# Small matrix products ahead of a recurrence, spread over parts of the TensorE array

## The chip, the cores and the metric

One core of a Trainium2 chip runs the whole program in one launch. The metric is the device time of an execution in microseconds (us). The engines are TensorE (PE; its weight loads are shown as PEld), VectorE (DVE), ScalarE (ACT), GpSimd (POOL) and SyncE (SP, which issues most of the transfers).

## What is computed

Two layers of an encoder on 768 tokens of width 1024 (a prompt of 512 and a sample of 256). Layer 0 runs differential attention and a bidirectional RWKV-7 time mixing side by side; layer 1 is a dilated sliding-window attention; each layer ends in a feed-forward part. The change lies in the time mixing. Its core in the reference, for 8 heads of width 64, once forwards and once backwards:

```python
def icl_rate(a0, a1, a2):
    return jax.nn.sigmoid((a0 + (xa @ a1) @ a2).astype(f32))

def step(st, inp):
    r_t, w_t, k_t, v_t, kk_t, a_t = inp
    sa = jnp.einsum('bhvk,bhk->bhv', st, -kk_t)
    st = (st * w_t[:, :, None, :] + sa[..., None] * (kk_t * a_t)[:, :, None, :]
          + v_t[..., None] * k_t[:, :, None, :])
    y = jnp.einsum('bhvk,bhk->bhv', st, r_t)
    return st, y
```

The decay `w_t` and the rate `a_t` come from two-stage ("low-rank") gates of the tokens.

## The kernel before

**The recurrence in chunks.** The kernel cuts the 768 tokens into 12 chunks of 64. Within a chunk the steps of the scan become matrix products, if the inverse of a unit triangular 64x64 matrix is at hand for every chunk, head and direction. `rkv` prepares all that for four pairs of heads (pair j, heads at partitions 0 to 63 and 64 to 127), and `rwkv` runs the recurrence later from what was stored to DRAM.

**For each pair and direction** (`operand_set`, j = 0 to 3, "f" then "b"): `stage` makes the second stage of the decay's and the rate's gate, two products each (512 and 256 tokens), in the PSUM bank `st`, each with a sigmoid on ACT (L671). `operands` makes the chunk operands on DVE and POOL, among them KB (L606) and AL (L608, L609). `store` sends them to DRAM. `products` makes A = KB^T AL per chunk and head, a 64x64 product (L632), six of one head in the one bank `pr`; ACT copies the 32x32 diagonal blocks into G (L645) and the other block into AO (L648). One more product in `pr`, `bonus`, ends a pair.

**The inverses** (`invert`) are made in three groups of 16 (pair, chunk) for both heads and directions: group 0 holds pair 0 and chunks 0 to 3 of pair 1, group 1 reaches to chunk 7 of pair 2, group 2 to the end of pair 3. DVE turns G into M (L729 forwards, L730 backwards), and then inverts 128 blocks of 32x32 at once, row after row: a multiplication (L737) and a sum (L739) for each, 48 of each in a group, a strict chain. Four transposes (L750, L751) end a group; L751 writes into M's memory. ACT and POOL copy them into TS, Tif and Tib (L769). Then PE makes the block off the diagonal: for each direction and head 16 products of 32x32 of AO with TS in the one bank `iv`, a copy to Hs (L774), 16 more of Hs with Ti, and a copy into Ti (L779), eight batches with a copy behind each. The result goes to DRAM.

**What sets the order.** PE has much else to do meanwhile: the projections of r, k, v, of the attention's values and of its q and k, in bank `gm` (line L83, three products in float32r for one exact product). The program is written in plain order; the scheduler of the Tile framework puts each engine's instructions into one fixed order by its own reckoning at build time, so an engine waits at the next instruction of its list even if a later one could run. The eight PSUM banks are given out by use: `iv` 1, `gm` 4, `uv` 1, `st` 1, `pr` 1.

In the code below, `self.mm` is a matrix product (L83 or, for plain float32, L84), `self.bank(tag)` takes the next PSUM bank of a use, `P` is 128.

## Time and profile before

| | us |
|---|---|
| three runs | 2135.32, 2132.63, 2128.2 |
| median | 2132.63 |
| span of the profiled execution | 2132.5 |
| PE busy | 2047.4 |
| DVE busy | 1392.7 |
| ACT busy | 906.3 |
| POOL busy | 882.1 |

In the span, the products of `pr` lie between 103 and 337 us, those of `iv` between 271 and 475, and the recurrence begins at 502. "Busy" sums up the instructions of an engine; a stretch of the span has to be looked at by itself, since the engines' loads differ from stage to stage. In a row of a timeline the bracket at the end tells how long the engine stood idle before it and what it was then released by. PE's rows are its matrix products; `x12` means twelve records one after another, and a float32 product has two records, a float32r one has one.

### The profile page before, as it was taken

The numbers are of one execution on the slowest core, as the hardware profiler recorded it, in microseconds if no ns is written. First come the engines' busy times: TensorE is split into PE (matmuls) and PEld (weight loads), VectorE is DVE, ScalarE is ACT, GpSimd is POOL, SyncE is SP. The second block draws the span as 40 slices with busy tenths as digits, with TensorE's granted clock in tenths as the row PEclk, the third lists the DMA queues.
The fourth block names the chain that finished last, engine by engine and source line by source line (L and its number), as shares of the span: only waits on it lengthen the run. The fifth ranks groups of instructions, "written<-read, shape, count | busy, mean of one in ns | idle before, by whom it ended". The sixth has DMA issues, their size and how long they took to land. (4 is left out here: it accounts for less than half of the span.)

```text
span 2132.5 us, 33757 instructions
## 1 busy us (share of the span) xinstructions
PE 2047.4 (96%) x13270; PEld 1775.0 (83%) x13270; DVE 1392.7 (65%) x2147; ACT 906.3 (43%) x1703; POOL 882.1 (41%) x833
## 2 busy tenths in 40 slices
PE   7999999999998989999999999999998999999998
PEld 7767666777887779999999998888677999999997
DVE  5456987956679567566666667643567666666665
ACT  5467555356655254433333334222454433333332
POOL 3345331552113157543434535443137544543442
PEclk9999989998999999999999999999998999999999
DMA  4334325114356312211221235221121121111124
GB/s 155 84 78 92 90 65 162 43 26 132 95 165 179 124 51 79 79 60 60 77 72 70 76 132 195 71 70 39 50 109 60 62 87 70 69 70 60 60 80 148
DMA packets 150228, 189.01 MB, mean 89 GB/s; under 512 B 95927, under 2 KB 107785, under 8 KB 150069
## 3 DMA queue, kind: packets, MB, share of 16 engines
q1 hardware_dynamic: 126880, 168.00, 24.6%
q10 hardware_dynamic: 20372, 12.03, 2.0%
q0 software_dynamic: 2816, 6.83, 1.0%
q8 instruction: 104, 1.70, 0.3%
q14 instruction: 56, 0.45, 0.1%
HBM read 150.20 MB, written 36.23 MB: 87 GB/s over the span
## 5 line engine op out<-in xcount | busy, mean ns | idle before, releaser
L83 PE MATMUL gm<-xh,w 128*128 128x384 f32 x896 | 249.6, 343 | 2.9 <-ACT xh L139 2.9
L140 DVE TENSOR_TENSOR wl<-wraw,wh 128x1024 fp32r<-128x1024 f32 (+1 forms) x96 | 128.0, 1334 | 153.0 <-ACT wh L139 150.7
L83 PE MATMUL gm<-T,w 128*128 128x384 f32 x1032 | 203.8, 340 | 6.6 <-ACT w L139 6.0
L83 PE MATMUL gm<-xh,wh 128*128 128x256 f32 (+3 forms) x640 | 206.1, 346 | 1.2 <-ACT pad L489 0.8
L83 PE MATMUL gm<-xl,wh 128*128 128x256 f32 (+3 forms) x640 | 204.5, 345 | 0.0
L83 PE MATMUL gm<-xh,wl 128*128 128x256 f32 (+3 forms) x640 | 203.0, 344 | 0.0
L140 DVE TENSOR_TENSOR w<-S,w 128x512 fp32r<-128x512 f32 x176 | 168.5, 959 | 43.8 <-ACT w L139 36.3
L83 PEld LDWEIGHTS gm<-T,w 128*128 128x128 f32 x1032 | 184.3, 188 | 11.4 <-ACT w L139 7.2
L139 ACT CAST wh<-wraw 128x1024 fp32r<-128x1024 f32 (+1 forms) x103 | 107.5, 1045 | 163.0 <-PE gm L83 88.3
L139 ACT CAST w<-S 128x512 fp32r<-128x512 f32 x176 | 108.8, 621 | 155.0 <-POOL S L291 54.6
L83 PEld LDWEIGHTS gm<-xh,w 128*128 128x128 f32 x896 | 167.9, 192 | 7.8 <-ACT xh L139 3.5
L139 ACT CAST w<-wraw 128x512 fp32r<-128x512 f32 x126 | 76.5, 620 | 207.9 <-PE gm L83 138.3
L83 PE MATMUL gm<-xl,w 128*128 128x384 f32 x448 | 153.6, 343 | 4.0 <-DVE xl L140 4.0
L293 POOL TENSOR_TENSOR S<-wraw,S 128x512 f32<-128x512 f32 x42 | 62.8, 1496 | 204.5 <-DVE w L140 204.5
L140 DVE TENSOR_TENSOR w<-wraw,w 128x512 fp32r<-128x512 f32 x126 | 116.8, 944 | 39.6 <-ACT w L139 39.6
L83 PE MATMUL sc<-xh,w 128*128 128x384 f32 x512 | 140.8, 336 | 1.1 <-DVE u L330 1.1
L83 PEld LDWEIGHTS gm<-xh,wh 128*128 128x128 f32 (+1 forms) x640 | 119.0, 193 | 21.0 <-issue 4.9
L83 PEld LDWEIGHTS gm<-xl,wh 128*128 128x128 f32 (+1 forms) x640 | 118.3, 193 | 21.3 <-issue 9.1
L83 PEld LDWEIGHTS gm<-xh,wl 128*128 128x128 f32 (+1 forms) x640 | 118.5, 193 | 20.8 <-issue 7.9
L392 DVE TENSOR_TENSOR acc<-acc,ob 128x512 f32<-128x512 f32 x128 | 87.4, 683 | 67.0 <-PE ob L83 65.8
L83 PE MATMUL sc<-T,w 128*128 128x384 f32 x552 | 112.6, 343 | 6.0 <-DVE sil L330 2.6
L348 POOL TENSOR_TENSOR sil<-sil,v 128x384 f32<-128x384 f32 x44 | 46.9, 1065 | 163.3 <-DVE v L330 163.1
(502 smaller groups left out, 5312.1 us busy)
## 6 DMA issues: line engine op xcount, KB each, us to landing
wraw<-in_gate SPq DMA_DIRECT2D x44, 512.0 KB, 3.4
wraw<-in_down SPq DMA_DIRECT2D x44, 512.0 KB, 3.5
wraw<-in_up SPq DMA_DIRECT2D x40, 512.0 KB, 3.4
wraw<-in_wqk SPq DMA_DIRECT2D x20, 512.0 KB, 3.5
wraw<-in_wo SPq DMA_DIRECT2D x14, 512.0 KB, 4.1
wraw<-in_wrkv SPq DMA_DIRECT2D x12, 512.0 KB, 3.5
KB<-pkKB SPq DMA_DIRECT2D x24, 256.0 KB, 3.5
pkx<-x SPq DMA_DIRECT2D x12, 512.0 KB, 3.4
```

The costliest lines, as they stand in the source:

```text
L83: return self.nc.tensor.matmul(o, a, b, start=start, stop=stop)
L139: self.nc.scalar.copy(out=hi, in_=x)
L140: (eng or self.nc.vector).tensor_tensor(out=lo, in0=x, in1=hi.bitcast(F32), op=ALU.subtract)
L293: eng.tensor_tensor(out=s2, in0=a12, in1=s2, op=ALU.subtract)
L348: nc.gpsimd.tensor_tensor(out=o, in0=o, in1=a[0], op=ALU.mult)
L392: nc.vector.tensor_tensor(out=accs[t][:, fs], in0=accs[t][:, fs], in1=os[t, f], op=ALU.add)
```

## The change

It does three things in layer 0, none elsewhere.

1. `products`: six chunks of both heads fill one `pr` bank, head 0 and head 1 in turn, so that neighbouring products use different halves of the array's rows and columns. Two steps of 12 products replace four of 6. The copies are the same in number and size and follow behind both heads.
2. `invert`: the 64 products of a kind (16 for each direction and head) fill one `iv` bank in turn over the four, and Hs is copied once, from 128 partitions. The copies into Ti stay four.
3. `stage`: the decay's product for a split of the tokens is followed by the rate's for the same split, the first in bank `st`, the second in bank `pr`; the rate's weights and hidden rows are packed with the directions swapped, so that the two use different halves of the array's rows.

```diff
         def products(j, d, AL, RH, KB, KK):
             ba = 0 if d == "f" else 1
-            def step(par, c0, n):
-                rr = slice(64 * par, 64 * par + 64)
+            def step(c0, n):
                 b = self.bank("pr")
                 for c in range(n):
-                    self.mm(b[rr, c * 64:c * 64 + 64], KB[rr, c0 + c], AL[rr, c0 + c])
-                bv = b[:, 0:n * 64].rearrange("p (c t) -> p c t", t=64)
+                    for rr in (slice(0, 64), slice(64, P)):
+                        self.mm(b[rr, c * 64:c * 64 + 64], KB[rr, c0 + c], AL[rr, c0 + c])
+                for par in range(2):
+                    copies(b[:, 0:n * 64].rearrange("p (c t) -> p c t", t=64), par, c0, n)
+
+            def copies(bv, par, c0, n):
                 i = 12 * j + c0
...
-            for a in ((0, 0, 6), (1, 0, 6), (0, 6, 6), (1, 6, 6)):
-                step(*a)
+            for c0 in (0, 6):
+                step(c0, 6)
...
         def stage(j, d):
             di = "fb".index(d)
-            rr = slice(64 * di, 64 * di + 64)
-            out = []
-            for n, w, b0 in (("w", self.w2, "w0_"), ("a", self.a2, "a0_")):
-                x = tile("s" + n)
-                for s0, S in SPLIT:
-                    o = self.bank("st")
+            out = [tile("sw"), tile("sa")]
+            of = (("w", self.w2, "w0_", di, "st"), ("a", self.a2, "a0_", 1 - di, "pr"))
+            for s0, S in SPLIT:
+                os = [self.bank(tag) for *_, tag in of]
+                for o, (n, w, b0, half, _) in zip(os, of):
+                    rr = slice(64 * half, 64 * half + 64)
                     self.mm(o[:, :S], w[rr, j * P:(j + 1) * P], self.hid[n][rr, s0:s0 + S])
+                for x, o, (n, w, b0, *_) in zip(out, os, of):
                     nc.scalar.activation(out=x[:, s0:s0 + S], in_=o[:, :S], func=AF.Sigmoid, bias=col(b0 + d, j))
-                out.append(x)
             return out
...
+        hb = self.bank("iv")
+        for c in range(16):
+            for di, ba, bb, ra, rb in parts:
+                self.mm(hb[rb, c * 32:c * 32 + 32], AO[ra, c], TS[ra, c])
+        nc.scalar.copy(out=Hs.rearrange("p c t -> p (c t)"), in_=hb)
+        hb = self.bank("iv")
+        for c in range(16):
+            for di, ba, bb, ra, rb in parts:
+                self.mm(hb[ra, c * 32:c * 32 + 32], Hs[rb, c], Ti[di][rb, c, 32 * bb:32 * bb + 32])
         for di, ba, bb, ra, rb in parts:
-            hb = self.bank("iv")
-            for c in range(16):
-                self.mm(hb[rb, c * 32:c * 32 + 32], AO[ra, c], TS[ra, c])
-            nc.scalar.copy(out=Hs[rb].rearrange("p c t -> p (c t)"), in_=hb[rb])
-        for di, ba, bb, ra, rb in parts:
-            hb = self.bank("iv")
-            for c in range(16):
-                self.mm(hb[ra, c * 32:c * 32 + 32], Hs[rb, c], Ti[di][rb, c, 32 * bb:32 * bb + 32])
             nc.scalar.copy(out=Ti[di][ra, :, 32 * bb:32 * bb + 32], in_=hb[ra].rearrange("p (c t) -> p c t", c=16))
...
-    a["wla"] = cols_tile(np.concatenate([i["a1_f"], i["a1_b"]], 1))[0]
+    a["wla"] = cols_tile(np.concatenate([i["a1_b"], i["a1_f"]], 1))[0]
...
-    a["a2"] = np.concatenate([i["a2_f"], i["a2_b"]])
+    a["a2"] = np.concatenate([i["a2_b"], i["a2_f"]])
```

The remaining lines of the diff take comments away; line numbers move by three from `stage` on and by four behind `invert`. The scheduler's order of the whole of layer 0 moves with the change; in layer 1, from its feed-forward part on, it is the same. Numbers in the names below only tell tiles apart; line numbers are those of the kernel each piece comes from.

PE, before, the last products of pair 3 (`pr` from AL and KB, backwards) among the products of the third gate (`st`):

```order
L84 MATMUL pr_354_2737<-AL_348_2705,KB_350_2707 64x64 x6
L84 MATMUL st_395_3251<-g2a_494,hg_3167 128x512
L84 MATMUL st_395_3251<-pad0_280,hh_3234 128x512
L84 MATMUL pr_355_2747<-AL_348_2705,KB_350_2707 64x64 x6
L84 MATMUL st_397_3257<-g2a_494,hg_3167 128x512
L84 MATMUL st_397_3257<-pad0_280,hh_3234 128x512
L84 MATMUL pr_356_2757<-AL_348_2705,KB_350_2707 64x64 x6
L84 MATMUL st_399_3263<-g2a_494,hg_3167 128x512
L84 MATMUL st_399_3263<-pad0_280,hh_3234 128x512
L84 MATMUL pr_372_3042<-rk_277,kfb_352_2709 128x2 x6
```

PE, before, a little later, the first off-diagonal products of group 1 (`iv` from TS and AO) among projections (`gm`):

```order
L83 MATMUL gm_423_3411<-wh_410_3289,xh_2_89 128x512
L83 MATMUL gm_423_3411<-wl_411_3290,xh_2_89 128x512
L83 MATMUL gm_423_3411<-wh_410_3289,xl_3_90 128x512
L83 MATMUL gm_423_3411<-wh_410_3289,xh_2_89 128x512
L84 MATMUL iv_284_2212<-TS_280_2192,AO_175_1264 32x32 x16
L83 MATMUL gm_423_3411<-wl_411_3290,xh_2_89 128x512
L83 MATMUL gm_423_3411<-wh_410_3289,xl_3_90 128x512
```

So all of pair 3 stands ahead of group 1's off-diagonal products. PE after, at the same place:

```order
L84 MATMUL st_363_3214<-pad0_280,hh_3191 128x512
L84 MATMUL iv_266_2191<-TS_262_2171,AO_171_1266 32x32 x64
L84 MATMUL pr_327_2695<-AL_322_2673,KB_324_2675 64x64 x12
L84 MATMUL st_365_3220<-g2a_494,hg_3124 128x512
L84 MATMUL st_365_3220<-pad0_280,hh_3191 128x512
L83 MATMUL gm_389_3368<-wh_370_3234,xh_2_89 128x512
L83 MATMUL gm_389_3368<-wl_371_3235,xh_2_89 128x512
```

The first block of pair 3 backwards (`pr_327`) stands right behind the 64 products of group 1. PE after, the second block (`pr_328`) and what is ahead of it:

```order
L84 MATMUL iv_267_2257<-Tif_264_2173,Hs_263_2172 32x32 x2
L84 MATMUL iv_267_2257<-Tib_265_2174,Hs_263_2172 32x32 x2
L84 MATMUL pr_328_2714<-AL_322_2673,KB_324_2675 64x64 x12
L84 MATMUL st_367_3226<-g2a_494,hg_3124 128x512
L84 MATMUL st_367_3226<-pad0_280,hh_3191 128x512
```

It stands behind the second batch of group 1's off-diagonal products, the one that reads Hs.

DVE, before, from the last transposes of group 1 to the first rows of group 2:

```order
L750 STREAM_TRANSPOSE tm_279_2087<-X_278_2086 64x1024
L751 STREAM_TRANSPOSE M_277_2085<-X_278_2086 64x1024
L750 STREAM_TRANSPOSE tm_279_2087<-X_278_2086 64x1024
L751 STREAM_TRANSPOSE M_277_2085<-X_278_2086 64x1024
L679 COPY bon_79<-pr_372_3042 128x6x2
L729 STREAM_TRANSPOSE M_357_2767<-G_258_1979 64x1024
L730 STREAM_TRANSPOSE M_357_2767<-G_258_1979 64x1024
L737 TENSOR_TENSOR tm_359_2769<-X_358_2768,M_357_2767 128x1 x2
L739 TENSOR_REDUCE X_358_2768<-tm_359_2769 128x1 x2
```

DVE, after, at the same place:

```order
L753 STREAM_TRANSPOSE tm_261_2066<-X_260_2065 64x1024
L754 STREAM_TRANSPOSE M_259_2064<-X_260_2065 64x1024
L603 TENSOR_SCALAR kfb_326_2677<-sa_316_2654,cols_115,omka_272 128x768
L605 SCALAR_TENSOR_TENSOR sa_316_2654<-kk_276_2403,sa_316_2654 128x768
L732 STREAM_TRANSPOSE M_329_2733<-G_243_1967 64x1024
L606 TENSOR_TENSOR KB_324_2675<-sa_316_2654,sw_315_2653 128x768
L733 STREAM_TRANSPOSE M_329_2733<-G_243_1967 64x1024
L740 TENSOR_TENSOR tm_331_2735<-X_330_2734,M_329_2733 128x1 x2
L742 TENSOR_REDUCE X_330_2734<-tm_331_2735 128x1 x2
```

Between the transposes and M there now stand two instructions that lead to KB of pair 3 backwards (L603, L605), and KB itself (L606) between M's two halves.

PE, before, the last of the projections (`gm`) ahead of the recurrence, with the attention's transposes (`tr`) and scores (`sc`) behind:

```order
L83 MATMUL gm_683_4673<-xh_2_89,wh_685_4676 128x256
L83 MATMUL gm_683_4673<-xl_3_90,wh_685_4676 128x256
L83 MATMUL gm_683_4673<-xh_2_89,wl_686_4677 128x256
L87 MATMUL tr_487_3782<-ident_113,o2_483_3770 128x128 x3
L84 MATMUL iv_371_3020<-Tib_363_2877,Hs_361_2875 32x32 x16
L87 MATMUL tr_487_3782<-ident_113,o2_483_3770 128x128
L84 MATMUL sc_544_4052<-k_514_3865,q_512_3863 128x512
L84 MATMUL sc_544_4052<-l_515_3866,q_512_3863 128x512
```

PE, after, at the same place:

```order
L83 MATMUL gm_649_4630<-xl_3_90,wh_651_4633 128x256
L83 MATMUL gm_649_4630<-xh_2_89,wl_652_4634 128x256
L87 MATMUL tr_453_3739<-ident_113,o2_449_3727 128x128 x4
L84 MATMUL sc_515_4033<-k_479_3821,q_477_3819 128x512
L84 MATMUL sc_515_4033<-l_481_3823,q_477_3819 128x512
L84 MATMUL sc_517_4040<-k_480_3822,q_478_3820 128x512
L84 MATMUL sc_517_4040<-l_481_3823,q_478_3820 128x512
```

The last off-diagonal batch stood behind the last projection before and now stands far ahead of it. From the last projection to the recurrence's first product there are 43 rows between them before and 32 now.

## Rows read from the trace of the kernel before

**Rows 1.** the page, busy us with the share of the span, and instructions
```profile
PE 2047.4 (96%) x13270; PEld 1775.0 (83%) x13270; DVE 1392.7 (65%) x2147; ACT 906.3 (43%) x1703; POOL 882.1 (41%) x833
```

**Rows 2.** windows: stretch, us, busy PE, PEld, DVE, ACT, POOL, clock, DMA share, GB/s
```profile
0.00:204.00 204.00, 187.83 (x1100) 148.81 (x1101) 109.56 (x129) 115.28 (x201) 84.25 (x60) 0.97 0.39 104
204.00:262.00 58.00, 52.99 (x313) 40.06 (x313) 57.41 (x123) 30.68 (x60) 20.73 (x11) 0.91 0.33 73
262.00:290.00 28.00, 24.25 (x168) 17.55 (x169) 22.32 (x24) 21.16 (x36) 14.05 (x11) 0.79 0.46 117
290.00:338.00 48.00, 47.40 (x397) 32.16 (x397) 43.56 (x106) 22.93 (x43) 12.39 (x9) 0.98 0.39 84
338.00:352.00 14.00, 11.79 (x34) 6.76 (x32) 9.18 (x8) 11.21 (x13) 5.89 (x7) 0.63 0.37 117
352.00:428.00 76.00, 73.17 (x599) 59.29 (x599) 70.17 (x151) 30.03 (x42) 32.26 (x33) 1.00 0.27 86
470.00:502.00 32.00, 28.94 (x142) 20.68 (x141) 15.94 (x45) 14.34 (x41) 10.37 (x31) 0.68 0.27 75
```

**Rows 3.** groups of DVE, 204 to 428 us: names, shapes, count, busy us, mean ns
```profile
L737 DVE TENSOR_TENSOR tm<-X,M 128x1 f32<-128x1 f32 (+15 forms) x144 | 81.5, 593 | 1.0
L739 DVE TENSOR_REDUCE X<-tm 128x1 f32<-128x1 f32 (+15 forms) x144 | 43.4, 326 | 1.1
```

**Rows 4.** timeline of DVE at both hand-overs: start us, us, engine, line, operation
```profile
270.62 1.90 DVE L751 STREAM_TRANSPOSE M<-X 64x1024 f32<-64x1024 f32 x1
...
289.98 0.21 DVE L737 TENSOR_TENSOR tm<-X,M 128x1 f32<-128x1 f32 x2
...
342.69 1.91 DVE L751 STREAM_TRANSPOSE M<-X 64x1024 f32<-64x1024 f32 x1
...
349.52 1.24 DVE L729 STREAM_TRANSPOSE M<-G 64x1024 f32<-64x1024 f32 x1 [4.71 <-ACT TS L769]
...
352.12 0.23 DVE L737 TENSOR_TENSOR tm<-X,M 128x1 f32<-128x1 f32 x2
```

**Rows 5.** timeline of PE: small products, each with the next instruction
```profile
103.38 0.91 PE L84 MATMUL pr<-AL,KB 64*64 64x64 f32 x12
104.21 0.39 PE L83 MATMUL gm<-xh,wh 128*128 128x256 f32 x1
...
503.87 0.68 PE L84 MATMUL pp<-AL,KB 64*64 64x64 f32 x16 [0.78 <-DVE LR L968]
504.48 0.51 PE L84 MATMUL sc<-k,q 128*128 128x512 f32 x1
...
427.06 1.19 PE L84 MATMUL iv<-TS,AO 32*32 32x32 f32 x32
428.19 0.71 PE L84 MATMUL ob<-va,pT 128*128 128x128 f32 x4
```

**Rows 6.** timeline of PE: the first product of the recurrence
```profile
502.02 1.06 PE L84 MATMUL pp<-RH,KB 128*128 128x128 f32 x8
```

**Rows 7.** line 774, the Hs copies: min/median/max ns, first and last start
```profile
L774 ACT COPY Hs<-iv x12: 571/577/581, 279.2 to 450.2; 32x512 f32<-32x512 f32 x12
```

**Rows 8.** timeline of PE, behind the wait for AL of pair 0
```profile
132.39 1.54 PE L84 MATMUL pr<-AL,KB 64*64 64x64 f32 x12 [3.47 <-DVE AL L609]
133.86 1.22 PE L84 MATMUL st<-hw,w 64*128 64x256 f32 x2
...
142.10 0.28 PE L83 MATMUL gm<-xh,wh 128*128 128x256 f32 x1
142.22 0.39 PE L83 MATMUL gm<-xh,wl 128*128 128x512 f32 x1
142.46 0.28 PE L83 MATMUL gm<-xl,wh 128*128 128x256 f32 x1
```

**Rows 9.** timeline of ACT ahead of group 0
```profile
200.07 1.28 ACT L671 ACT_TABLE_LOAD   x1
...
202.08 0.79 ACT L645 COPY G<-pr 32x128 f32<-32x128 f32 x2
```

## The prediction

> **What bounds the kernel now.** I read the page's busy times first. TensorE (PE) is busy in 96% of the span [rows 1], so at first sight every microsecond taken from it comes back. That share is an average, and the change touches only the first 475 us, so I cut that part into stages with the windows view [rows 2]. Up to 204 us PE is the fullest engine, 187.8 of 204. From 204 to 428 us the 32-row inversions run on VectorE (DVE), three groups one after another: 57.4 of 58 us busy in the rows of group 0, 43.6 of 48 in group 1's, 70.2 of 76 in group 2's. PE is 84 to 99% busy there too, but with projections that no one awaits at once, and at 0.63 and 0.79 of its clock in the two stretches between the groups. The view of DVE's groups of instructions says what fills it: 144 multiplications and 144 reductions of the substitution, 124.9 us in one chain [rows 3]. So two things run side by side, a PE queue and a DVE chain, and what decides is which of them arrives last where they meet: at the products that feed a group (bank pr), and at the off-diagonal products behind it (bank iv).
>
> The DVE timeline shows the two hand-overs [rows 4]. Group 0's last transpose ends at 272.5 and the next group's rows start at 290.0: 17.5 us. Group 1's ends at 344.6 and the rows of group 2 start at 352.1: 7.5 us, 4.7 of it a wait for ScalarE's (ACT's) TS copies. This hand-over is short because the last products of pair 3 had long been made. Behind group 2 the iv products start at 427.06 [rows 5], the recurrence's first product at 502.02 [rows 6]. Of the 1630 us behind it the change alters nothing, and PE bounds them [rows 1], so the recurrence's start carries the end: a shift there is a shift of the time. The profiled span, 2132.5, and the median of the runs, 2132.63, agree, so the sum is made on 2132.5 and nothing is added around it.
>
> **What the change saves on PE.** *Products:* a block of 6 products (12 records) runs from 103.38 to the next instruction at 104.21, 0.83 us, 69 ns for a record with its share of the entry [rows 5]. There are 32 blocks: 26.6 us. The recurrence's own 64x64 products already alternate between heads: 16 records from 503.87 to 504.48, 0.61 us, 38 ns for a record [rows 5]. By that price 16 blocks of 24 records are 16 x 0.91 = 14.6 us, a gain of 12 (0, if they take turns, to 13, if the price is just half). *Off-diagonal products:* 32 records from 427.06 to 428.19, 1.13 us, 35 ns each; 24 blocks are 27.1 us. Four tiles now alternate. Nothing in [rows 5] shows four, so I bound it: no gain (27), halved once as with the two heads (about 13), or twice (7). I take 13, a gain of 14 (0 to 20). *ACT* saves 9 of 12 Hs copies, 9 x 0.577 = 5.2 us [rows 7]; ACT is half idle there [rows 2], so this counts as nothing by itself. *Stage:* the order on PE does not bring the two gates' products together: other products stand between w's (bank st) and a's (bank pr). Products that are not neighbours share nothing, so I give this 0. Its cost is that the one pr bank now serves 16 products of a more; that price lies in the first term below. In all 26 us (0 to 33) of PE's time, were it all on the path.
>
> The Trainium skill ("TensorEngine Tiling (Array Packing)", Gotcha 1: PSUM Pressure) says that different row tiles cannot access one PSUM bank at the same time, which would take the gain of the products away, since both heads still fill one bank. By that rule the 12 us would be 0. The recurrence's products of two heads at 38 ns [rows 5], made in one bank too, speak against it; it comes back as a rival.
>
> **Why I don't count that gain.** The whole order moves, so I follow the chain from station to station.
>
> 1. *Group 0's start (its first rows, at 204 us).* On PE the products ahead of it are 7 blocks of 24 records in place of 14 of 12: 14 x 0.83 less 7 x 0.91, 5.2 us saved. But the order puts 22 projections of 512 and 21 of 256 columns more ahead of it; by the 0.24 and 0.12 us from start to start in [rows 8] that is 5.3 + 2.5 = 7.8 us. Two products of the gates' second stage fewer stand ahead of it, one of 512 and one of 256 columns, some 2 us by the 1.22 of one of 256 at half clock [rows 8], so no net work is left on either side. What may be won: PE stood 3.47 us for AL of pair 0's backward direction, and at 132.39 the block took 1.54 in place of 0.91 us, half clock [rows 8]; this AL now comes earlier on DVE. What may be lost: the pr bank is waited for by a's sigmoids. I take -4 (between -9, the wait and the slow stretch behind it both gone, and +3, one ACT copy queue behind a sigmoid and its table load, 200.07 to 202.08, [rows 9]).
>
> 2. *Hand-over of group 0 to 1.* Before: 17.5 us. Now KB of pair 2's backward direction stands on DVE behind the group's last transposes, and both its product blocks stand on PE behind iv of group 0; G's copies follow, then M. The chain counted as in the next item is 20 to 22 us; I take +4 (0 to +6).
>
> 3. *Hand-over of group 1 to 2.* This is the largest term. Before: all of pair 3's products stand on PE ahead of group 1's iv, M could start as soon as the TS copies let go of it. Now, from the order: DVE makes KB of (pair 3, backward) behind the transposes; PE has 64 iv products, then the first block of (pair 3, backward), then the projections and 64 more iv products that wait for Hs, and only then the second block; ACT has Hs, six copies, three bank copies of other work, the Ti copies and then the six copies of that second block, for which M waits. Counted from the end of the last transpose: TS copies 4.9 us (344.6 to 349.52, [rows 4]); the first iv batch 2 to 4; Hs 0.6 [rows 7]; six copies at about 0.4 (0.39 for the two of [rows 9]) 2.4; three copies as wide as Hs 1.7, while PE does the products up to the second batch; four Ti copies as long as Hs's 2.3, later by up to 2 if the second batch is; six copies 2.4; a transpose of M 1.24 [rows 4]. That is 17.5 to 21.5 us in place of 7.5. I take 18.5, +11 (+6, if ACT's copies of other work hide in PE's time, to +14). DVE has KB's chain of about 4 us to do in it that before lay among the rows, and this comes off the rows: it is in the lower end.
>
> 4. *Group 2's end to the recurrence.* Before: 75 us, of which 470 to 502 is the tail of the attention, 32 us with PE at 0.68 of its clock and 3 us of gaps [rows 2]. iv's eight batches with a copy behind each are now two, and more projections are left for this stretch: the last of them stands 33 rows ahead of the recurrence's first product, 44 before. Behind it there are 12 scores of 512, 12 value products and 22 transposes, before 16, 20 and 26. So less attention stands alone, without projections to fill its waits. If that tail shrinks with them (to 0.75, 0.60 and 0.85, together some 0.73), 32 becomes 23. -9 (-13 to 0).
>
> 5. *Behind.* What the tail lost runs later among the recurrence, about 3 us of scores, value products and transposes: +3.
>
> Sum: -4 + 4 + 11 - 9 + 3 = +5, 2137.5 us. The own range of this case adds up ends that don't all fall together: about 2126 to 2150. PE's 26 us become waits of PE at the first iv products of each group. The cover of the gain is the DVE chain; if DVE ran with less work in its rows, the gain would appear.
>
> **Rivals.**
>
> *The gain passes through.* PE at 96% is the bound all along, DVE's idle time at the hand-overs is only PE's lateness, and G comes early enough. For it: at 338 to 352 us DVE is 9.2 of 14 busy and PE 11.8 [rows 2], and the whole span is PE. Against: in the groups' rows DVE is 91 to 99% busy, which no faster PE shortens. Time: 2132.5 - 26 = 2106 (2099 to 2120).
>
> *The hand-overs cost more than the tail returns.* Place: pair 3's second block behind group 1's second iv batch. Price: items 2 and 3 at their upper ends, +6 and +14, and the tail not shorter since it is paced by ACT, DVE and POOL in turn and not by PE's work (0), with +3 behind and nothing at group 0: +23, 2155. It decides from the point where group 2's rows start later than about 365 us in the span.
>
> *One bank lets no two heads in.* Then the products keep their 69 ns and iv 35: 5.2 us more ahead of group 0, some 2.5 more in each hand-over: 2137.5 + 10.2, about 2148. This is also how the change could fail to do what it says; the stage's pairs, not neighbours in the order, do so in every case.
>
> **How the numbers follow.** About 0.3% (6.4 us) is what a measurement of this kernel can tell from no change, so "same" is 2126 to 2139. My case has 0.47: 0.09 faster, 0.25 same, 0.13 slower, since its centre is near the upper edge. Passing through has 0.27, all faster. Dearer hand-overs have 0.19 and the serial bank 0.07, both slower. Faster 0.36, same 0.25, slower 0.39. The predicted time is that of my case, 2137.5. The range must leave out at most 2 in 10: down to 2104, which holds most of the passing through, and up to 2156, which holds the dearer hand-overs. That is 2104 to 2156; my case alone is 2126 to 2150.
>
> **What would show it.** In the trace of the changed kernel: PE's waits at the first iv product of each group, 5 to 20 us each; DVE's gap between the last transpose of group 1 and the first multiplication of group 2 at 16 to 22 us; group 2's iv products between 430 and 442; the recurrence's first product at 495 to 510; a block of 24 products in about 0.9 us, 64 iv products in 2 to 4. I am wrong if the recurrence starts before 490, with PE busy through 204 to 428 us (passing through), or if group 2's rows start before 355 us; and on the products if a block of 24 takes 1.4 us or more.

## The result and the profile after

The changed kernel takes 2149.18 us (median, 2142.92 to 2153.72), the kernel before 2133.07 on the same chip (2128.20 to 2135.32): a ratio of 1.0084, 95% interval 1.0062 to 1.0107. It is slower by 16 us by the medians, where +5 was forecast. The profiled executions have spans of 2146.2 and 2132.5 us, and what follows accounts for those 13.7 us.

The page of the kernel after, PE's and the other engines' busy us, which answers to [rows 1]:

```profile
PE 2037.3 (95%) x13270; PEld 1760.2 (82%) x13270; DVE 1393.3 (65%) x2147; ACT 902.8 (42%) x1694; POOL 886.3 (41%) x833
```

PE is busy 10 us less, in a span that is 13.7 us longer. The windows view (columns as in [rows 2]) cuts both kernels at three points: the recurrence's first product (`pp`), the first product that the recurrence makes in the banks of the attention's scores (`sc<-SUV,LK`, so the attention has ended), and the first product of the feed-forward. Before:

```profile
0.00:502.00 502.00, 465.57 (x3108) 357.14 (x3109) 348.93 (x630) 271.40 (x484) 202.55 (x191) 0.93 0.33 88
502.00:604.30 102.30, 99.93 (x1327) 83.26 (x1325) 65.40 (x156) 65.28 (x180) 17.55 (x56) 1.00 0.43 121
604.30:787.40 183.10, 166.82 (x1790) 142.16 (x1790) 136.27 (x209) 79.04 (x167) 55.06 (x54) 0.96 0.44 140
```

After:

```profile
0.00:498.80 498.80, 441.18 (x3086) 330.95 (x3087) 351.27 (x630) 264.70 (x471) 204.38 (x191) 0.89 0.34 88
498.80:609.80 111.00, 105.94 (x1350) 86.98 (x1348) 64.74 (x156) 67.81 (x186) 18.99 (x56) 1.00 0.42 116
609.80:800.10 190.30, 174.29 (x1789) 149.20 (x1789) 135.85 (x207) 79.83 (x167) 53.85 (x54) 0.95 0.42 132
```

The stretch that the change rewrites became 3.2 us shorter. PE was relieved of 24.4 us in it (465.57 to 441.18) and handed back 21.2: its idle time grew from 36.4 to 57.6 us, and the mean clock fell from 0.93 to 0.89. Since the clock has two levels, 1.2 and 2.4 GHz, a mean of 0.93 is 14% of the stretch at the lower one, about 70 us, and 0.89 is 22%, about 110 us (each to some 5 us). The loss lies in the two stretches behind, 8.7 and 7.2 us (the remaining 1.0 us lies later still). The diff does not touch their code, but they belong to layer 0, and the scheduler gave their instructions another order: before, PE makes no score between the first `pp` product and the first `pp<-AL,KB`; after, it makes two pairs of scores there (499.65 to 501.34).

That the small products do alternate, the PE timeline of the kernel after shows (start us, us from first start to last end, line, tiles, shape, count, and in brackets the wait ahead of it):

```profile
199.29 0.91 PE L84 MATMUL pr<-AL,KB 64*64 64x64 f32 x24
200.13 1.12 PE L84 MATMUL st<-hw,w 64*128 64x512 f32 x2
...
260.75 0.24 PE L84 MATMUL iv<-TS,AO 32*32 32x32 f32 x2 [4.12 <-ACT TS L772]
...
436.12 1.24 PE L84 MATMUL iv<-TS,AO 32*32 32x32 f32 x122 [0.42 <-ACT TS L772]
...
498.83 1.06 PE L84 MATMUL pp<-RH,KB 128*128 128x128 f32 x8
...
605.68 0.71 PE L84 MATMUL ob<-va,pT 128*128 128x128 f32 x4
...
609.14 0.69 PE L87 MATMUL tr<-ident,o 128*128 128x128 f32 x2 [2.75 <-DVE o L904]
609.76 1.12 PE L84 MATMUL sc<-SUV,LK 128*64 128x64 f32 x16
```

A block of 24 records of `pr` starts 0.84 us ahead of its successor, 35 ns for each against 69 [rows 5]. The last 122 of the 128 records of group 2's first `iv` batch take 1.24 us, about 10 ns each against 35 [rows 5]. At full clock the products so save 16 x (2 x 0.83 - 0.84) = 13 us and the off-diagonal ones 24 x 1.13 - 6 x 1.24 = 20 us.

The waits of PE from 0 to 530 us, after (us in total, times, longest us):

```profile
PE iv L84 <- ACT TS L772: 12.9, 10, 4.1
PE pr L84 <- issue: 7.3, 2, 6.2
...
PE pr L84 <- DVE KB L606: 5.6, 4, 3.3
```

Before, no wait of an `iv` product for TS was longer than 0.4 us. DVE's timeline after at both hand-overs, beside [rows 4]:

```profile
199.77 0.20 DVE L740 TENSOR_TENSOR tm<-X,M 128x1 f32<-128x1 f32 x2
...
259.74 1.89 DVE L754 STREAM_TRANSPOSE M<-X 64x1024 f32<-64x1024 f32 x1
...
282.64 0.20 DVE L740 TENSOR_TENSOR tm<-X,M 128x1 f32<-128x1 f32 x2
...
335.92 1.89 DVE L754 STREAM_TRANSPOSE M<-X 64x1024 f32<-64x1024 f32 x1
...
344.94 1.07 DVE L606 TENSOR_TENSOR KB<-sa,sw 128x768 f32<-128x768 f32 x1
...
362.41 1.24 DVE L733 STREAM_TRANSPOSE M<-G 64x1024 f32<-64x1024 f32 x1 [16.40 <-ACT G L648]
363.76 0.23 DVE L740 TENSOR_TENSOR tm<-X,M 128x1 f32<-128x1 f32 x2
```

Group 0's rows start at 199.8 instead of 204. The first hand-over takes 21.0 us (261.63 to 282.64) instead of 17.5, the second 25.9 (337.81 to 363.76) instead of 7.5. What M waited for in the second is in ACT's timeline after (ACTq rows are transfers that ACT itself issues):

```profile
346.72 0.58 ACT L815 COPY vv<-gm 128x512 f32<-128x512 f32 x1 [2.37 <-DMA pkg<-vv]
...
347.70 0.58 ACT L777 COPY Hs<-iv 128x512 f32<-128x512 f32 x1 [0.40 <-PE pr L84]
348.31 0.95 ACT L648 COPY G<-pr 32x192 f32<-32x192 f32 x2
...
354.85 0.58 ACT L815 COPY s<-gm 128x512 f32<-128x512 f32 x1 [2.49 <-DMA pkg<-s]
...
355.83 1.16 ACT L783 COPY Tif<-iv 32x512 f32<-32x512 f32 x2 [0.40 <-ACT s L815]
...
357.07 1.01 ACTq L789 DMA_DIRECT2D pkTi<-Tif  x2
...
358.27 1.76 ACTq L789 DMA_DIRECT2D pkTi<-Tib  x2
360.08 1.02 ACT L648 COPY G<-pr 32x192 f32<-32x192 f32 x2 [1.89 <-issue]
...
361.43 0.95 ACT L648 COPY G<-pr 32x192 f32<-32x192 f32 x2
```

As forecast, the second block's G copies stand behind Hs, other banks and the Ti copies. Three things stand in that queue besides: the four issues of the Ti transfers, which hold the G copies up by 1.89 us, an issue of 0.33 us behind each copy of other work, and two waits of ACT, 2.37 and 2.49 us. In both, the profile names as releaser a transfer to DRAM of the tile (`vv`, `s`) that the copy was to write next. Why KB of the last direction came only at 344.94, here between the transposes of group 1 and M, is read from ACT's sigmoids of the rate in the groups view, 0 to 400 us (idle time just before them, and its releaser). After:

```profile
L675 ACT ACTIVATE sa<-pr,cols 128x512 f32<-128x512 f32 (+1 forms) x16 | 9.3, 581 | 19.9 <-PE pr L84 19.9
```

The kernel before has 1.8 us of idle time on that line. The rate's products now take their turn in the one bank `pr`, behind the chunk products and their copies, and ACT stood 19.9 us for them; sa leads to KB, whose eighth and last product on DVE started at 320.5 before and at 344.9 after.

### The profile page after: what moved, and what is told of

It reads as the page before. It is cut to its first block, busy times and chain, and to the rows that moved or that the text cites. A ratio compares the mean times of both kernels' runs of the same rounds, so it can differ in the third digit from the quotient of the medians.

```text
span 2146.2 us, 33739 instructions
## 1 busy us (share of the span) xinstructions
PE 2037.3 (95%) x13270; PEld 1760.2 (82%) x13270; DVE 1393.3 (65%) x2147; ACT 902.8 (42%) x1694; POOL 886.3 (41%) x833
## 5 line engine op out<-in xcount | busy, mean ns | idle before, releaser
L139 ACT CAST wh<-wraw 128x1024 fp32r<-128x1024 f32 (+1 forms) x103 | 107.5, 1046 | 166.6 <-PE gm L83 96.6
L139 ACT CAST w<-S 128x512 fp32r<-128x512 f32 x176 | 109.0, 621 | 151.8 <-POOL S L291 52.7
L139 ACT CAST w<-wraw 128x512 fp32r<-128x512 f32 x126 | 76.1, 620 | 208.4 <-PE gm L83 138.2
```

The lines of the kernel that those rows point to most:

```text
L139: self.nc.scalar.copy(out=hi, in_=x)
```

## Experiments

Two theories on which part costs the time: A, the rate's products in the bank `pr` (part 3 of the change) push the last products behind group 1; B, the alternation itself (parts 1 and 2) harms. Two on what sets the recurrence's start: C, DVE's chain of inversions, as the prediction has it; D, PE's list, with the chain only making PE wait. E: more but shorter small products bring the clock down. F and G came later: less or more work for PE carries through to the end in full (F), or the list has room (G).

**One part at a time.** e1 is the change without part 3: `stage()` and the columns of wla and a2 are those of before.

```diff
-            for s0, S in SPLIT:
-                os = [self.bank(tag) for *_, tag in of]
-                for o, (n, w, b0, half, _) in zip(os, of):
+            for n, w, b0 in (("w", self.w2, "w0_"), ("a", self.a2, "a0_")):
+                x = tile("s" + n)
+                for s0, S in SPLIT:
+                    o = self.bank("st")
```

> The change without its third part: the rate's second-stage products stay in bank st, products and off-diagonal products alternate as in the change. Theory A (the rate's products in the one pr bank push pair 3's last products behind group 1's off-diagonal products, and group 2 starts late): all products of pair 3 stand ahead of group 1 again, the hand-over from group 1 to 2 falls from 26 us to 8 to 12 us, and the time is 15 to 30 us below the change's, 2120 to 2134 us. Theory B (alternating does the harm itself: PE's batches wait for all TS copies at once and its clock falls): the time stays within 5 us of the change's, 2144 to 2154 us, whatever the hand-over does.

2132.86 us, ratio 1.0007 (0.9994 to 1.0020). Its stretch up to the recurrence, in the windows view:

```profile
0.00:497.30 497.30, 441.82 (x3100) 334.08 (x3101) 354.36 (x632) 265.11 (x475) 207.74 (x191) 0.90 0.34 90
```

PE is relieved of 23.8 us as in the whole change, the second hand-over takes 9.4 us, and group 2 ends at 392.4 instead of 427.6. The recurrence starts 4.7 us earlier, and the time is that of before: theory A's numbers came, and in the change without part 3 the alternation costs nothing. It gains nothing either. Group 2's 35 us did not carry to the recurrence's start.

e2 is part 3 alone, on the kernel before:

```diff
-            for n, w, b0 in (("w", self.w2, "w0_"), ("a", self.a2, "a0_")):
+            of = (("w", self.w2, "w0_", di, "st"), ("a", self.a2, "a0_", 1 - di, "pr"))
+            for s0, S in SPLIT:
+                os = [self.bank(tag) for *_, tag in of]
```

> Only the third part of the change: the rate's second-stage products go to bank pr, everything else as in the kernel before. In the order, the last four blocks of pair 3 stand behind group 1's first off-diagonal products, as in the change. Theory A: the hand-over from group 1 to 2 is 18 us or more in place of 7.5, and the time is 2140 to 2155 us though nothing alternates. Theory B: no batches of 64, no harm: within 6 us of the kernel before.

2174.87 us, 1.0206 (1.0185 to 1.0227): +43. The hand-overs take 32.2 and 39.5 us. Its row of the rate's sigmoids, in the view shown above for after:

```profile
L672 ACT ACTIVATE sa<-pr,cols 128x512 f32<-128x512 f32 (+1 forms) x16 | 9.3, 582 | 33.4 <-PE pr L84 33.4
```

And its PE timeline behind group 1, small products alone:

```profile
370.33 1.91 PE L84 MATMUL iv<-TS,AO 32*32 32x32 f32 x32
372.17 1.54 PE L84 MATMUL pr<-AL,KB 64*64 64x64 f32 x12
...
384.40 0.91 PE L84 MATMUL pr<-AL,KB 64*64 64x64 f32 x12
...
391.23 0.91 PE L84 MATMUL pr<-AL,KB 64*64 64x64 f32 x12
...
396.01 1.19 PE L84 MATMUL iv<-Tif,Hs 32*32 32x32 f32 x32
397.14 0.91 PE L84 MATMUL pr<-AL,KB 64*64 64x64 f32 x12
```

Four blocks that group 2's rows need come one by one between group 1's `iv` batches, from 372 to 398 us. This is theory A's mechanism, larger than in the change (39.5 us in place of 25.9), and the time lies above the range that A gave. PE's gain of part 3 was to be that w's and a's products run together; other products stand between them in the order, and nothing was gained.

e3 is part 1 alone, e4 part 2 alone (both in the diff ahead of the prediction):

```diff
-            for a in ((0, 0, 6), (1, 0, 6), (0, 6, 6), (1, 6, 6)):
-                step(*a)
+            for c0 in (0, 6):
+                step(c0, 6)
```

> Only the first part of the change: products of both heads alternate in one pr bank. Theory A: PE saves 12 us, of which little passes through since DVE's groups set the pace; pair 3 stays ahead of group 1; 2122 to 2134 us. Theory B: same or slower, 2130 to 2145 us. If the whole gain on PE counted it would be 2120 us.

2142.78 us, 1.0062 (1.0042 to 1.0082). That is 11 us more than before, in theory B's range and not in A's, with `pr` used as before and a second hand-over of only 6.3 us. Its recurrence starts at 491.9, 10 us earlier than before, and the feed-forward at 794.3, 7 us later: the alternation of part 1 alone costs time too, all of it behind the recurrence's start, and e1, which has part 1 as well, does not show that cost.

```diff
-        for di, ba, bb, ra, rb in parts:
-            hb = self.bank("iv")
-            for c in range(16):
+        hb = self.bank("iv")
+        for c in range(16):
+            for di, ba, bb, ra, rb in parts:
                 self.mm(hb[rb, c * 32:c * 32 + 32], AO[ra, c], TS[ra, c])
```

> Only the second part of the change: 64 off-diagonal products alternate over four tiles and Hs is copied once. Theory A: group 2's end to the recurrence shortens from 75 us to 62 to 70 us since eight batches with copies become two; the hand-overs stay; 2120 to 2132 us. Theory B: PE's wait for all TS copies costs 5 to 10 us in each group and the time is 2135 to 2150 us.

2128.13 us, 0.9983 (0.9971 to 0.9995), the one version with the whole computation below before: some 3.5 us out of 20 that PE saves. The time is in A's range. Its recurrence starts at 485.6, 16 us earlier, but not because the stretch from group 2's end to the recurrence shrank to 62 to 70 us, as A had it: group 2 ended 27 us earlier, at 401.0, and that stretch grew to 84.6. So the parts do not add up: by the medians of one chip +11, -4 and +43 us alone, +1 for the first two together, and +16 for all three on theirs.

**Bank or order.** e5 keeps the order and the halves of part 3, on the kernel before, with both gates in `st` again:

```diff
-                os = [self.bank(tag) for *_, tag in of]
-                for o, (n, w, b0, half, _) in zip(os, of):
+                for x, (n, w, b0, half) in zip(out, of):
+                    o = self.bank("st")
```

> Only the third part, but without its second bank: decay and rate take turns split by split and use opposite halves of the rows, both in bank st. Theory A (the shared pr bank does the harm): all products of pair 3 stand ahead of group 1's off-diagonal products, hand-over from group 1 to 2 under 14 us, time 2125 to 2142 us. Theory B (the turn-taking does the harm, since the rate's sigmoid now comes between the decay's): 2150 us or more, as in the third part alone (2175).

2153.94 us, 1.0093 (1.0065 to 1.0120). The order came as A had it (pair 3 ahead of group 1, a second hand-over of 11.6 us), the time as B had it. Of e2's 43 us the shared bank makes 22 (the sigmoids' idle time is 6.6 instead of 33.4 us, group 2 ends at 418.7, ahead of before). The other 21 come without it, in a kernel where w and a are made in turn. I had no mechanism for those: PE is busy 475.67 us up to the recurrence, 10 more than before at a clock of 0.91, and which instruction starts that the profile did not tell me. About half of the 21 us comes up to the recurrence's start (511.7), half in the stretch from the attention's end to the feed-forward (194.2 in place of 183.1 us).

e6 is the whole change with a second `pr` bank, taken from the projections:

```diff
-        with C.phase("h1", gm=4, uv=1, st=1, pr=1) as hp:
+        with C.phase("h1", gm=3, uv=1, st=1, pr=2) as hp:
```

> The whole change, with two pr banks and three for the projections in place of one and four. Theory A: the products of pair 3 stand ahead of group 1's off-diagonal products, the hand-over falls to about 10 us, and the time is 2125 to 2140 us, 10 to 25 below the change. Theory B (harm by the alternating batches or by a projection bank less): 2145 us or more.

2143.94 us, 1.0048 (1.0032 to 1.0064). The rate's sigmoids idle 1.6 us, the last KB starts at 305.7, the second hand-over takes 6.5 us and group 2 ends at 388.1, 43 us earlier than in the change. All that returned 5 us by the medians, 8 by the ratios, and the time lies between the ranges of A and B. (It also takes a bank from the projections, and its profiled execution is 7 us below its median.) So in the whole change the shared bank makes the late hand-over, as A says, but taking it away returns only a third to a half of the loss. What makes the rest is not shown here: the gates in turn, which cost time alone (e5), or the bank that the projections lack.

**What sets the recurrence's start.** Half of the substitution's rows left out, in the kernel before (e7) and in the change (e8):

```diff
-        for i in range(1, 32):
+        for i in range(1, 32, 2):
```

> The kernel before with every second row of the substitution left out (rows 1, 3, 5, ... alone), so that VectorE's chain in each group is about half as long. Theory C (inverses' chain sets the start of the recurrence): some 50 us or more faster, under 2085 us. Theory D (TensorE's own list up to the last projection sets it; the chain only makes TensorE wait): the recurrence starts at most 20 us earlier, 2110 to 2133 us.

> The changed kernel with every second row of the substitution left out, as in the kernel before with half the rows. Theory D: with the chain short TensorE waits less for it, the time at half clock ahead of the last projection falls from 99 to under 60 us, and the change gains over the kernel before with half the rows: 15 to 30 us less than that. Theory E (the small alternating products themselves bring the clock down): the time at half clock stays above 85 us and the time is no more than 5 us below the kernel before with half the rows.

e7: 2125.80 us, 0.9971 (0.9959 to 0.9982). e8: 2137.81, 1.0027 (1.0012 to 1.0041). Up to the recurrence, e7:

```profile
0.00:484.80 484.80, 459.54 (x3110) 353.44 (x3111) 294.22 (x494) 272.14 (x485) 205.37 (x194) 0.95 0.35 91
```

and e8:

```profile
0.00:491.50 491.50, 436.15 (x3102) 328.17 (x3102) 301.00 (x495) 266.01 (x476) 202.88 (x194) 0.90 0.35 91
```

With 55 us less on DVE, e7's group 2 ends 50 us earlier (377.0), the recurrence starts 17 us earlier and the time falls by 7, in D's range. So the recurrence's start does not follow DVE's chain, and C falls. In e8 PE has 23 us less to do than in e7, and stands idle 55 us instead of 25. D expected the gain to appear there, and it did not: e8 is 12 us above e7. Both signs of E came: the mean clock of 0.90 (0.95 in e7) is about 98 us at the lower level, where E had more than 85 and D less than 60. But e8's second hand-over is late as well, 36.4 us, so this pair does not show that the clock is the cause.

**More and less for PE.** e9 makes each chunk product twice, in the kernel before, 32 x 0.83 = 26.6 us:

```diff
-                for c in range(n):
+                for c in [*range(n), *range(n)]:
```

> The kernel before with every product of KB and AL made twice (the second time over the first): 26.6 us more of TensorE's time, where the change wants to save. Theory F (TensorE's own list carries the recurrence's start in full): 2152 to 2162 us. Theory G (the list has room at these places, since it waits for the other engines' operands there anyway): no more than 10 us above the kernel before.

e10 leaves out one of the three float32r products of the attention's q and k projections:

```diff
-                for j, (w, x) in enumerate(((0, xh), (0, xl), (1, xh))):
+                ps = ((0, xh), (1, xh)) if two else ((0, xh), (0, xl), (1, xh))
+                for j, (w, x) in enumerate(ps):
...
-            b = self.proj(self.A["wqk0"][4 * i + j], xh, xl)
+            b = self.proj(self.A["wqk0"][4 * i + j], xh, xl, two=True)
```

> The kernel before with one of the three float32r products left out in the projections of the attention's q and k (64 instructions of 512 and 64 of 256 columns, 23 us of TensorE's time; these stand behind and between the inverses and wait for little). Theory F: 2107 to 2114 us. Theory G, if it holds for the whole stretch and not for the small products alone: 2125 us or more.

e9: 2153.81 us, 1.0102 (1.0071 to 1.0134). e10: 2140.24, 1.0046 (1.0031 to 1.0061). Work that is added to PE came through for the most part, 22 us of 26.6, in F's range; the work that was taken away, 20 us by PE's busy time, gave nothing, and 8 us were lost on top, as G had it. e9's first stretch shows that the time came as F had it and the path did not:

```profile
0.00:513.10 513.10, 484.59 (x3486) 377.60 (x3486) 347.55 (x633) 272.66 (x485) 205.75 (x194) 0.94 0.33 87
```

The recurrence starts only 11 us later. PE stands idle 8 us less ahead of it (28.5 instead of 36.4), its clock is a little higher (0.94 instead of 0.93), and the other 9.5 us come behind, where no product was added. e10's windows, cut at the same three points:

```profile
0.00:484.50 484.50, 445.98 (x2947) 339.65 (x2947) 345.61 (x628) 270.11 (x482) 206.43 (x191) 0.90 0.35 91
484.50:597.70 113.20, 108.18 (x1361) 88.17 (x1360) 66.56 (x158) 66.92 (x183) 18.10 (x56) 0.99 0.43 115
597.70:788.40 190.70, 173.19 (x1789) 146.58 (x1788) 136.66 (x206) 78.23 (x166) 54.61 (x54) 0.96 0.41 131
```

Its recurrence starts 17.5 us earlier, with no small product changed: up to there the 20 us did come through. Then the next two stretches take 303.9 us instead of 285.4 and give all of it back. They are what decides: in the kernel before they take 285.4 us, less than in any other kernel of this study (288.1 to 303.9), whether PE's work was raised, lowered or left alone. So neither F nor G holds as it was put. Each of these kernels was given its own order of layer 0, and no run kept the order of these two stretches: that the kernel before has an order that happens to suit them is a rival that stands untested.

**Do the waits for TS take the gain?** e11 is e1, e12 is e4, each with the transposes that feed TS made first:

```diff
-            nc.vector.transpose(out=TT[h], in_=xv)
             nc.vector.transpose(out=TN[h], in_=xv.rearrange("p i j -> p j i"))
+        for h, rv in ((slice(0, 64), False), (slice(64, P), True)):
+            xv = X[h, ::-1, ::-1] if rv else X[h]
+            nc.vector.transpose(out=TT[h], in_=xv)
```

> The change without its third part, and the four transposes that end a group in another order: the two that feed TS first, so that ACT makes all four TS copies first. If TensorE's waits for TS at the batches of 64 take back the gain: those waits fall from 11 to under 5 us, and the time falls by 5 to 12 us against the same kernel without it (2132.9). If the clock and other waits take it back: within 4 us of 2132.9.

> The second part of the change alone (2128.1), with the transposes that feed TS first. If waits for TS matter: 2118 to 2125 us. If not: 2125 to 2132 us.

e11: 2136.66 us, 1.0029 (1.0012 to 1.0045). e12: 2136.16, 1.0022 (1.0006 to 1.0038). PE's wait for TS in e11, from the waits view:

```profile
PE iv L84 <- ACT TS L774: 7.1, 5, 3.2
```

In e1 it was 11.1 us in 7 waits. The waits shrank, though not to under 5 us, the recurrence started at 489.1 in place of 497.3, and the time rose by 4 us. e12's time, 8 us above e4's, lies above both ranges, and its recurrence starts 8 us later than e4's. In these two kernels, making the waits shorter brought nothing.

## Why the prediction was right and wrong

The range held the time, and the sign was right; the size was off by 12 us (2149.2 against 2137.5). The sign was right by luck: the four terms up to the recurrence add up to +2, and the recurrence started 3.2 us earlier; the loss came from the fifth term, which had +3 and measured +16.9. The order of the first three stations was read rightly, but the step that joins them to the end, start of a group to start of the recurrence to end of the span, is wrong (see the premises). By the prediction's own steps:

- **The saving on PE.** 26 us were taken, with 12 for the products and 14 for the off-diagonal blocks. Measured are 13 and 20: four tiles halve the time twice, the upper end of the bounds. Nothing for part 3 was right. That the saving would not reach the end was right as well: e1 relieves PE of 23.8 us and keeps the time.
- **Term 1, group 0's start: -4.** Measured -4.8; the wait of 3.47 us for AL is gone. Right.
- **Term 2, first hand-over: +4.** Measured +3.5. Right.
- **Term 3, second hand-over: +11, at most +14.** Measured +18.4 (25.9 in place of 7.5), beyond the upper end, and the order behind it was as described. What it mis-sized is ACT's queue: it counted copies alone. Between them stood ACT's wait for the transfer of `vv`, which held Hs up by 2.0 us, the wait for that of `s` (2.5), three issues of other work (1.0) and the Ti issues (1.9); the TS copies took 5.9 us in place of 4.9 (337.8 to 343.7). These 8.4 us on the 17.5 of its lower sum make the 25.9. PE's half clock added nothing to it: the batch of `iv` took 1.91 us, where the sum had 2 to 4.
- **Term 4, group 2's end to the recurrence: -9.** Group 2 ended at 431.5, only 3.9 us later, since the rows themselves became shorter, by 6.1 us in group 0 and 7.7 in group 2, which the sum had at nothing or in a lower end. In group 0 one KB left the rows, and the multiplications took 24.9 us in place of 30.3; in group 2 DVE no longer stood 5.0 us for ACT's `wh` (L139). From the first `iv` product of group 2 to the first `pp` it took 68.3 in place of 75 us, -6.7. Right within its bounds, and for the reason given: from the last projection to the first `pp` it took 20.4 us (478.48 to 498.83) in place of 29.8 (472.25 to 502.02), the tail's -9. The recurrence started at 498.83, where the four terms give 504.
- **Term 5, behind: +3.** This is the step that failed and the one that decides: it measured +16.9 (1630.5 us from the first `pp` to the end became 1647.4). Its first part, up to the end of the attention, grew by 8.7 us. The prediction priced the attention's remainder at PE's cost of its products. There are 14 more records of value products behind the start (104 for 90), 6 more of transposes (50 for 44) and one more pair of scores, by PE's busy time 4 us, near the price. Another 2.75 us are a wait at its end: the last value products start at 605.68, their transposes wait for DVE, and the recurrence gets the scores' banks at 609.76. The remaining 2 us are not accounted for; the recurrence's own products are the same in number. Before, PE did recurrence products between the last value products and their transposes, and there was no wait:

```profile
598.61 0.71 PE L84 MATMUL ob<-va,pT 128*128 128x128 f32 x4
...
603.93 0.44 PE L87 MATMUL tr<-ident,o 128*128 128x128 f32 x2
604.30 0.69 PE L84 MATMUL sc<-SUV,LK 128*64 128x64 f32 x16
```

  The second part grew by 7.2 us with the same number of instructions, and PE busy 7.5 us more in them. A clock of 0.95 in place of 0.96 makes some 2 us of it, an estimate from the two means. The rest stays open: this part varies between 183 and 194 us over the 14 kernels, with code that is the same in all and an order that is not. Its length goes with its clock: the three longest (192.2 to 194.2, in e3, e5 and e11) have means of 0.93 and 0.94, the four shortest (182.7 to 185.5, in e2, the kernel before, e7 and e1) have 0.96; e10, 190.7 at 0.96, is an exception. Which of the two makes the other was not tested.
- **What was to be seen.** The second hand-over (16 to 22 us forecast) took 25.9; group 2's `iv` products start at 430.57 (430 to 442), the recurrence's first at 498.83 (495 to 510), a block of 24 takes 0.91 us (1.54 at half clock): these came, the first too late. A batch of 64 `iv` products (2 to 4 forecast) takes 1.2 us, or 1.9 at half clock, once it runs. PE's waits at the first `iv` products did not come as forecast, 5 to 20 us each: none is longer than 4.1, 12.9 in all. PE's other waits at `pr` (7.3 and 5.6 us) and the lower clock stand beside them.
- **The premises.** "A shift there is a shift of the time" is wrong: e10, e11 and e3 start the recurrence 10 to 17.5 us earlier and are slower. "The cover of the gain is the DVE chain" is wrong as well: e6, e7 and e1 end group 2 by 35 to 51 us earlier than the kernel before and start the recurrence by 5 to 17 earlier, and in e8, with half the rows, the gain did not appear (it has a late hand-over of its own). What does stand ahead of the recurrence is in the code: its banks `cf`, `cb` and `pp` take the place of the three that the projections of q and k use, so it cannot start before the last of those. That alone does not set the start: it came 29.8 us behind the last projection in the kernel before, 20.4 in the change and 37 in e10. That what is saved ahead of the start only moves the attention's remainder behind it fits e10 and the change; it is argued, not shown.
- **The rivals.** Passing through (2106) falls with PE idle 21 us more. Dearer hand-overs (2155) was nearest in time, but by another way: the second hand-over was as dear as it said and group 2's rows started at 363.8, just short of its point of decision, while the tail did return 6.7 us. One bank that lets no two heads in falls with 0.84 us for a block of 24.

The Trainium skill ("TensorEngine Tiling (Array Packing)", Gotcha 1: PSUM Pressure) says that different row tiles cannot access one bank at once. Here two heads into one bank take half the time, and four 32-row tiles into one bank less than a third; the measurement decides against the rule for these tiles, which write to different partitions of the bank.

What is settled: without part 3 the loss is gone (e1 against the change), the bank that part 3 shares moves the last chunk products behind group 1 (e2, e6), and of the 33 us that parts 1 and 2 save at full clock none comes back when both are made (e1), 3.5 of 20 with part 2 alone (e4), and less than nothing with part 1 alone (e3). What stays open: why w and a made in turn cost some 20 us without the shared bank (e5), why part 1 alone costs 11, why the stretches behind the recurrence's start are shortest in the kernel before, and how much of that their order makes and how much the clock. A kernel that moves only the bank and keeps the old order of emission was not run.

## What to carry to other kernels

An engine at 96% of the span, fed by three others in an order that a scheduler sets, can take added work at nearly its price and need not give back removed work. To learn which it is, add some work and take some away, as in e9 and e10, ahead of tuning small products, and look in both at where the time moved and not only at its sum. Before a second use is put on a single-buffered bank, look for what stands behind that bank in both queues: here it cost 22 us alone (e2 against e5), for products that gained nothing. A start that moves earlier is worth something only if what was left undone ahead of it does not come back behind it, so a sum must be made to the next point where both lists have been emptied.

## What the runs showed of the hardware

Four 32x32 float32 tiles in turn ran at about 10 ns a record (122 in 1.24 us), where one tile took 35; I had taken 17.

The clock can stay low while PE is full. In e4 PE waited 4.24 us for AL, and small products and the third gate's plain float32 products came next. Its timeline at that place:

```profile
319.58 1.51 PE L84 MATMUL pr<-AL,KB 64*64 64x64 f32 x12 [4.24 <-DVE AL L609]
```

and its windows from there (columns as in [rows 2]):

```profile
318.00:325.00 7.00, 5.42 (x16) 2.35 (x16) 6.73 (x11) 1.27 (x3) 0.00 (x0) 0.50 0.77 139
325.00:332.00 7.00, 7.00 (x30) 3.73 (x29) 6.79 (x8) 2.29 (x5) 1.85 (x2) 0.50 0.11 39
332.00:340.00 8.00, 8.00 (x20) 3.31 (x20) 2.86 (x2) 6.36 (x11) 3.98 (x6) 0.50 0.26 82
...
356.00:366.00 10.00, 10.00 (x166) 7.79 (x164) 9.83 (x27) 5.75 (x10) 1.44 (x3) 1.00 0.66 160
```

The granted clock was 0.50, the lower level, from 317.8 to 355.4 us though PE was busy without a gap from 325 to 340. In this stretch the gate's product of 512 columns takes 2.07 us (at 321.02), and it took 1.13 just ahead of it (at 309.94), so the 38 us at the lower level may have cost up to 17, an estimate from these two, against 4.24 for the wait. The clock fell within that wait (315.3 to 319.6); that the wait brought it down, and what kept it down, was not tested.
